# Gate products placed between the small products of the chunks' solve, in a fixed order on TensorE

## The chip, the cores and the metric

The kernel runs on one core of one Trainium2 chip. The metric is the device time of one execution in microseconds (us); lower is better. The core's engines are TensorE (PE in the profile; its weight loads are listed as PEld), VectorE (DVE), ScalarE (ACT), GpSimd (POOL) and SyncE (SP), which issues the transfers. Each engine takes its instructions in a fixed order and waits for others through semaphores.

## The reference, cut to what matters

The program computes two layers one after the other on 512 tokens of 1024 features. The change lies in the second one, in the branch of RWKV-7 time mixing and in the gates of the same layer:

```python
def step(state, inp):
    r_t, w_t, k_t, v_t, kk_t, a_t = inp
    sa = jnp.einsum('bhij,bhj->bhi', state, -kk_t)
    state = (state * w_t[:, :, None, :]
             + sa[..., None] * (kk_t * a_t)[:, :, None, :]
             + v_t[..., None] * k_t[:, :, None, :])
    return state, jnp.einsum('bhij,bhj->bhi', state, r_t)
...
y_a = rwkv7_branch(z_rw, shift_mu, ...)
...
g_a, g_b = jnp.split(jax.nn.sigmoid(z_gate + b_gate), 2, axis=-1)
```

The gates multiply the outputs of the branches much later. Their projection `z_gate` has 16 panels of 128 features; it depends on the normed input alone, so its products may stand anywhere ahead of that.

## The kernel before

The recurrence over 512 tokens is done in eight chunks of 64 tokens, for four pairs of heads. Within a chunk it is a lower triangular system. `rwkv_prep` builds the matrices `Mt` and the values `VA` in SBUF. `rwkv_solve` solves the systems of all chunks at once, ahead of the scan: diagonal blocks of 32x32 are written to DRAM and read back so that each partition holds one block (`NT`), 31 steps on VectorE (L1385, L1387) invert them all, the inverses go back through DRAM (`zdd`) into `Wm` and `Mt`, and then TensorE joins the halves. That last part is the solve of this document: four groups of sixteen 32x32 products (L1407), four more of them (L1415), each followed by a copy out of PSUM, and for each of the four pairs of heads 32 products of 64x64 (L1421 and L1424 in turn). L1363, 16 such products, prepares the fourth pair's right side. `rwkv_scan` then goes through the eight chunks one after the other (L1460, L1464, L1469, L1478 on TensorE, L1462, L1474, L1476 on VectorE), and `rwkv_out` follows.

A product of fp32 is made of three: `panel` loads a panel of weights (two transfers of 256 KB, `wraw`), ACT casts its high part (L125), GpSimd subtracts for its low part (L128), and `mm3` (L135) multiplies high by high, by low, and low by high. For a panel of gates that is 8 x 3 = 24 products of 128x512 into one PSUM bank `f`; ACT's tanh (L2181) takes it out and SP stores it to `gtd` (L2182).

The order is made by a scheduler of the tile framework from the order in which the code is written. `K.fills` marks products as filling: they have a low priority and are put wherever TensorE would wait. Eight gate panels (`G2_AHEAD`) are such fills, every fourth through pool `fw` and the rest with `'main'`, written behind `dsa_index`, the choice of keys for the sparse attention branch. In that choice L1557/L1558 multiply on TensorE, `mask` is made on VectorE (L1563 to L1566) and its largest entries are taken in rounds of eight (L1569, L1570). `dg` (L178) and its four transposes (L1578) belong to it too. The other eight gate panels and the products of the cross attention's memory are fills as well, written later. Pool `fw` has two buffers for filling panels (`how=True`); with `'main'` a panel takes one of the main pool's three.

Of the kernel before, what the change touches and what calls it, by code (L numbers as in the profile page):

```python
# [11 lines left out]
F32 = mybir.dt.float32  # L12
F32R = mybir.dt.float32r
I32 = mybir.dt.int32
AF = mybir.ActivationFunctionType
# [3 lines left out]
P = 128  # L19
# [4 lines left out]
G2_AHEAD = 8  # L24
DI_BUFS = 6
# [20 lines left out]
class Core:  # L46
# [90 lines left out]
    def fills(self, items, hi, lo, n=T, how=True):  # L137

        self.filling = how
        for src, done in items:  # L140
            done(self.fm(src, hi, lo, n))
        self.filling = False

# [1208 lines left out]
def rwkv_solve(K, pool, Mt, VA, Wm):  # L1352

    nc, tc, a = K.nc, K.tc, K.a
    nd = tc.dram_tile([P, 1024], F32, name="ndd")
# [45 lines left out]
    Q = Wm.rearrange("p i c t -> p i (c t)")  # L1401
    for i in range(4):
        pq = K.acc(tags[i])
        for s in range(2):
            for c in range(8):
                o = (s * 8 + c) * 32
                nc.tensor.matmul(pq[96:128, o:o + 32], Mt[64:96, i, s, c, 32:64], T1[64:96, i, s, c], start=True,  # L1407
                                 stop=True, tile_position=(64, 96))
        K.copy(Q[96:128, i], pq[96:128])
    for i in range(4):  # L1410
        pz = K.acc(tags[i])
        for s in range(2):
            for c in range(8):
                o = (s * 8 + c) * 32
                nc.tensor.matmul(pz[64:96, o:o + 32], Q[96:128, i, o:o + 32], Mt[96:128, i, s, c, 32:64], start=True,  # L1415
                                 stop=True, tile_position=(96, 64))
        K.copy(Mt[64:96, i, :, :, 32:64], pz[64:96].rearrange("p (s c t) -> p s c t", s=2, c=8))
    for i in range(4):
# [8 lines left out]
        for c in range(8):  # L1427
            two(0, c)
            one(0, c)
            two(1, c)  # L1430
            one(1, c)
# [708 lines left out]
def block2(K, h3, xd, out):  # L2140
# [22 lines left out]
    K.dve_split = ()  # L2163
    DS = ExitStack()
# [5 lines left out]
    rwkv_solve(K, K.pool(I_, "inv"), Mt, VA, Wm)  # L2170
# [7 lines left out]
    def gate(f):  # L2178
        def done(z):
            t = rp.tile([P, 512], F32, name="gt", bufs=2)  # L2180
            nc.scalar.activation(t, z, AF.Tanh, scale=0.5, bias=K.pd["bg"][:, f:f + 1])  # L2181
            nc.sync.dma_start(gtd[f], t)  # L2182
        return done

    idx = dsa_index(K, dp, hhi, hlo)
    for f in range(G2_AHEAD):
        K.fills([(a["w2f"][22 + f], gate(f))], hhi, hlo, how=f%4==0 or 'main')
# [208 lines left out]
```

## Time and profile before

| | us |
|---|---|
| median of 3 runs | 2240.3 |
| lowest and highest run | 2227.89, 2240.66 |
| profiled execution | 2238.75 |
| its span, first to last instruction | 2237.0 |
| PE busy | 2086.9 (93%) |
| DVE busy | 1074.4 (48%) |
| ACT busy | 712.5 (32%) |
| POOL busy | 485.6 (22%) |
| chain that ended last: PE, DVE, DMA | 68%, 12%, 7% |
| granted TensorE clock over the span | 0.965 |

Busy time of TensorE counts records with modelled ends, and products overlap, so a rate is better read from the starts of successive instructions than from their lengths. [...] An fp32 product of the small kinds has two records.

The stages of interest are at these times of the span: the inverse on VectorE ends at about 1186 us, the solve's small products stand between 1208 and 1251, the scan from there to 1293.

### The profile page before, as it was taken

The page shows a single profiled execution, that of the slowest core. Times are in us where ns is not written, and L with a number is a line of the kernel's source. Part 1 is how long each engine was busy: PE and PEld are TensorE (multiplying, and loading weights), DVE is VectorE, ACT ScalarE, POOL GpSimd, SP SyncE. Part 2 cuts the span into 40 slices and gives each one's busy share as a digit, 9 for nine tenths or more (in the row PEclk, how much of TensorE's full clock was granted, in tenths as well). Part 3 has the DMA queues.
Part 4 walks back from the last instruction along what each step waited for, and adds up shares of the span by engine and source line. Part 5 has one row for each costly group of instructions (what it writes and reads, how often), then busy time and mean ns, then how long its engine had stood idle before and what let it go on. Part 6 is the DMA issues. An engine that isn't in the chain of part 4 may idle for free.

```text
span 2237.0 us, 28592 instructions
## 1 busy us (share of the span) xinstructions
PE 2086.9 (93%) x10252; PEld 1476.5 (66%) x10252; DVE 1074.4 (48%) x2554; ACT 712.5 (32%) x1507; POOL 485.6 (22%) x391
## 2 busy tenths in 40 slices
PE   7999899998999999979988999999997999999997
PEld 5777676686888888867777867777875433333332
DVE  5272226427764545475877656555445322222223
ACT  4253334433353434234532235543441110000102
POOL 2312331233133222233331121232131000000000
PEclk9899999999999999999998799999998999999999
DMA  5512332256242332133334342485257999999994
GB/s 174 162 47 67 94 97 73 67 173 230 73 138 96 98 99 95 58 112 107 101 116 108 105 162 91 156 260 167 94 187 264 403 416 413 413 415 414 413 415 182
DMA packets 203370, 411.39 MB, mean 184 GB/s; under 512 B 49192, under 2 KB 67752, under 8 KB 203096
## 3 DMA queue, kind: packets, MB, share of 16 engines
q1 hardware_dynamic: 200632, 400.08, 51.0%
q0 software_dynamic: 2592, 9.44, 1.1%
q8 instruction: 82, 1.34, 0.3%
q14 instruction: 64, 0.52, 0.1%
HBM read 371.46 MB, written 33.13 MB: 181 GB/s over the span
## 4 chain that ended last, share of the span: by engine, by line
PE 68%; DVE 12%; DMA 7%; issue 3%; ACT 3%; POOL 2%; SPq 0%; DVEq 0%; ACTq 0%; POOLq 0%
PE f L135 23%; PE f L2008 10%; PE s L2024 6%; PE acc L135 6%; PE s L135 6%; PE tp L135 2%; POOL w L128 2%; PE pv L269 1%; PE tp L261 1%; PE s L1934 1%; DMA wraw<-w2f 1%; PE pv L135 1%; ACT w L125 1%; DMA wraw<-wout 1%; PE pv L1934 1%
## 5 line engine op out<-in xcount | busy, mean ns | idle before, releaser
L128 POOL TENSOR_TENSOR w<-wraw,w 128x512 fp32r<-128x512 f32 x310 | 407.2, 1325 | 1074.1 <-ACT w L125 962.0
L125 ACT CAST w<-wraw 128x512 fp32r<-128x512 f32 (+1 forms) x446 | 261.6, 617 | 242.2 <-issue 51.7
L135 PE MATMUL f<-hhi,w 128*128 128x512 f32 (+1 forms) x832 | 281.0, 410 | 2.0 <-ACT w L125 0.7
L128 DVE TENSOR_TENSOR w<-wraw,w 128x512 fp32r<-128x512 f32 (+1 forms) x136 | 116.3, 856 | 189.6 <-ACT w L125 186.5
L2008 PE MATMUL f<-mw,xT 128*64 128x512 f32 x832 | 206.8, 594 | 0.0
L135 PE MATMUL f<-h2hi,w 128*128 128x512 f32 (+1 forms) x672 | 203.7, 384 | 0.3 <-POOL w L128 0.3
L135 PEld LDWEIGHTS f<-hhi,w 128*128 128x128 f32 x832 | 161.8, 200 | 35.1 <-issue 3.2
L135 PE MATMUL acc<-hhi,w 128*128 128x512 f32 (+1 forms) x512 | 169.3, 398 | 4.9 <-ACT w L125 1.9
L135 PE MATMUL f<-hlo,w 128*128 128x512 f32 (+1 forms) x416 | 170.0, 409 | 0.2 <-DVE hlo L187 0.2
L2008 PEld LDWEIGHTS f<-mw,xT 128*64 128x64 f32 x832 | 65.5, 137 | 124.6 <-issue 117.7
L135 PEld LDWEIGHTS f<-h2hi,w 128*128 128x128 f32 x672 | 125.2, 188 | 25.6 <-POOL w L128 0.5
L135 PE MATMUL f<-h2lo,w 128*128 128x512 f32 (+1 forms) x336 | 129.0, 384 | 0.0
L2024 PE MATMUL s<-mw,hT 128*64 128x512 f32 x416 | 121.8, 600 | 3.3 <-ACT hT L174 1.9
L135 PEld LDWEIGHTS acc<-hhi,w 128*128 128x128 f32 x512 | 96.3, 191 | 28.5 <-issue 4.3
L1966 POOL DMA_INDIRECT xs<-xnd,row x16 | 15.2, 953 | 423.3 <-DVE wraw L2000 171.0
L135 PE MATMUL acc<-hlo,w 128*128 128x512 f32 (+1 forms) x256 | 101.3, 396 | 0.0
L135 PEld LDWEIGHTS f<-hlo,w 128*128 128x128 f32 x416 | 83.1, 200 | 16.2 <-issue 1.4
L1895 DVE SCALAR_TENSOR_TENSOR hid<-hid,f 128x512 f32<-128x512 f32 x16 | 11.0, 688 | 160.3 <-ACT hid L1894 160.3
L1894 ACT ACTIVATE hid<-f,tg 128x512 f32<-128x512 f32 x16 | 11.0, 688 | 204.1 <-PE f L2008 204.1
L2024 PEld LDWEIGHTS s<-mw,hT 128*64 128x64 f32 x416 | 33.2, 136 | 59.6 <-issue 51.5
L135 PEld LDWEIGHTS f<-h2lo,w 128*128 128x128 f32 x336 | 63.1, 188 | 12.3
L2027 ACT ACTIVATE yhi<-s,tg 128x512 fp32r<-128x512 f32 x32 | 22.0, 688 | 150.8 <-PE s L2024 150.8
(743 smaller groups left out, 3991.4 us busy)
## 6 DMA issues: line engine op xcount, KB each, us to landing
mw<-wexp SPq DMA_DIRECT2D x310, 512.0 KB
w<-wexp SPq DMA_DIRECT2D x72, 512.0 KB
wraw<-wup SPq DMA_DIRECT2D x88, 256.0 KB
wraw<-w2f SPq DMA_DIRECT2D x76, 256.0 KB
wraw<-wgate SPq DMA_DIRECT2D x64, 256.0 KB
wraw<-wdown SPq DMA_DIRECT2D x44, 256.0 KB
wraw<-w1f SPq DMA_DIRECT2D x40, 256.0 KB
gated<-gt SPq DMA_DIRECT2D x28, 256.0 KB
```

Of the source, the lines that this page charges most:

```text
L125: nc.scalar.copy(hi[:, s], raw)
L128: eng.tensor_sub(lo[:, s], raw, hi[:, s].bitcast(F32))
L135: self.nc.tensor.matmul(out, l, r, start=start and i == 0, stop=stop and i == 2)
L261: nc.tensor.transpose(pt[:, off:off + P], Pt[s][i][:, j * P:(j + 1) * P], K.ident)
L269: one = lambda s: nc.tensor.matmul(o[64 * s:64 * s + 64, j * P:], v_of(j, s), ptS[s][:, at[j]:at[j] + n], start=start and j == 0, stop=sto ...
L1894: nc.scalar.activation(t, G, AF.Tanh, scale=half)
L1895: nc.vector.scalar_tensor_tensor(t, t, 1.0, G, op0=OP.add, op1=OP.mult)
L1934: K.nc.tensor.matmul(o, CT[:, b * P:(b + 1) * P], y[:, hs], start=start and i == 0, stop=i == len(items) - 1)
L1966: nc.gpsimd.indirect_dma_start(xs, None, self.xnd, bass.IndirectOffsetOnAxis(ap=row[:, 0:1], axis=0))
L2008: nc.tensor.matmul(o[64 * s:64 * s + 64], xT[:, kk, 64 * s:64 * s + 64], ws[s][k], start=kk == 0, stop=kk == 7)
L2024: nc.tensor.matmul(o[64 * s:64 * s + 64], hT[:, c, 64 * s:64 * s + 64], ws[s][c], start=c == 0, stop=c == 3)
L2027: nc.scalar.activation(yhi[:, hs], o, AF.Copy, scale=tg[:, 1:2])
```

## The change

A generator, `K.steps`, takes six of the gate panels (`G2_SOLVE`) and gives out their products three at a time. `rwkv_solve` gets it as `fill`. It takes one step (three products) at its beginning, and its function `between` then issues the small products in groups of sixteen (L1407, L1415) or eight (L1421/L1424), each followed by two steps, which is six gate products. With `tc.issue_after` each group stands behind the last gate product and the gate products behind the last of the group, so that this order on TensorE is fixed. All of their panels are loaded through pool `fw` of two buffers, and split by ACT and GpSimd. Only two gate panels are still written as fills behind `dsa_index`.

```diff
@@ -22,6 +22,7 @@
 G2_BUFS = 7
 BD_BUFS = 2
 G2_AHEAD = 8
+G2_SOLVE = 6
 DI_BUFS = 6
 DG_BUFS = 10
 DB_BUFS = 8
@@ -140,6 +141,23 @@
         for src, done in items:
             done(self.fm(src, hi, lo, n))
         self.filling = False
+
+    def steps(self, items, hi, lo):
+
+        pans = []
+        for n, (src, done) in enumerate(items):
+            self.filling = True
+            pans += [self.panel(s, 1024) for s, _ in items[len(pans):n + 2]]
+            o = self.acc("f")
+            self.filling = False
+            for k in range(8):
+                s = slice(k * P, (k + 1) * P)
+                w = [t[:, s] for t in pans[n]]
+                for i, (a, b) in enumerate(((0, hi), (0, lo), (1, hi))):
+                    self.last = self.nc.tensor.matmul(o, w[a], b[:, k, :], start=k == 0 and i == 0, stop=k == 7 and i == 2)
+                if k == 7:
+                    done(o)
+                yield
 
     def acc(self, name="acc"):
         if name not in self.pb:
@@ -1349,9 +1367,21 @@
         nc.sync.dma_start(kbd[:, :, p].rearrange("c p t -> p c t"), KB)
 
 
-def rwkv_solve(K, pool, Mt, VA, Wm):
+def rwkv_solve(K, pool, Mt, VA, Wm, fill):
+
 
     nc, tc, a = K.nc, K.tc, K.a
+    next(fill)
+
+    def between(products, n):
+        for i in range(0, len(products), n):
+            with tc.issue_after(K.last.ins):
+                for p in products[i:i + n]:
+                    K.last = p()
+            with tc.issue_after(K.last.ins):
+                next(fill, None)
+                next(fill, None)
+
     nd = tc.dram_tile([P, 1024], F32, name="ndd")
     zd = tc.dram_tile([P, 2, 1024], F32, name="zdd")
 
@@ -1399,21 +1429,18 @@
                                       ap=[[32, 32], [4096, 64], [1, 32]]))
     tags = ("acc", "pv", "s", "s")
     Q = Wm.rearrange("p i c t -> p i (c t)")
+    at = [(s, c, slice((s * 8 + c) * 32, (s * 8 + c) * 32 + 32)) for s in range(2) for c in range(8)]
     for i in range(4):
         pq = K.acc(tags[i])
-        for s in range(2):
-            for c in range(8):
-                o = (s * 8 + c) * 32
-                nc.tensor.matmul(pq[96:128, o:o + 32], Mt[64:96, i, s, c, 32:64], T1[64:96, i, s, c], start=True,
-                                 stop=True, tile_position=(64, 96))
+        between([lambda s=s, c=c, o=o: nc.tensor.matmul(pq[96:128, o], Mt[64:96, i, s, c, 32:64], T1[64:96, i, s, c],
+                                                        start=True, stop=True, tile_position=(64, 96))
+                 for s, c, o in at], 16)
         K.copy(Q[96:128, i], pq[96:128])
     for i in range(4):
         pz = K.acc(tags[i])
-        for s in range(2):
-            for c in range(8):
-                o = (s * 8 + c) * 32
-                nc.tensor.matmul(pz[64:96, o:o + 32], Q[96:128, i, o:o + 32], Mt[96:128, i, s, c, 32:64], start=True,
-                                 stop=True, tile_position=(96, 64))
+        between([lambda s=s, c=c, o=o: nc.tensor.matmul(pz[64:96, o], Q[96:128, i, o], Mt[96:128, i, s, c, 32:64],
+                                                        start=True, stop=True, tile_position=(96, 64))
+                 for s, c, o in at], 16)
         K.copy(Mt[64:96, i, :, :, 32:64], pz[64:96].rearrange("p (s c t) -> p s c t", s=2, c=8))
     for i in range(4):
 
@@ -1424,11 +1451,7 @@
         two = lambda s, c: nc.tensor.matmul(pu[s][64:128, c * 64:(c + 1) * 64], Mt[64:128, i, s, c, 0:64],
                                             LV[i][64:128, s, c * 64:(c + 1) * 64], start=True, stop=True,
                                             tile_position=(64, 64))
-        for c in range(8):
-            two(0, c)
-            one(0, c)
-            two(1, c)
-            one(1, c)
+        between([lambda f=f, s=s, c=c: f(s, c) for c in range(8) for f, s in ((two, 0), (one, 0), (two, 1), (one, 1))], 8)
         K.copy(Wm[:, i].rearrange("p c t -> p (c t)"), pw)
         for s in range(2):
             K.copy(VA[64:128, i, :, 64 * s:64 * s + 64], pu[s][64:128].rearrange("p (c t) -> p c t", c=8))
@@ -2161,13 +2184,24 @@
     rwkv_prep(K, K.pool(S, "prep"), hhi, hlo, Mt, VA, eC, xg, kbd, red, bvd)
     S.close()
     K.dve_split = ()
+
+    def gate(f):
+        def done(z):
+            t = rp.tile([P, 512], F32, name="gt", bufs=2)
+            nc.scalar.activation(t, z, AF.Tanh, scale=0.5, bias=K.pd["bg"][:, f:f + 1])
+            nc.sync.dma_start(gtd[f], t)
+        return done
+
     DS = ExitStack()
     dp = K.pool(DS, "dsa", "left")
     V = ExitStack()
     vp = K.pool(V, "solve")
     Wm = vp.tile([P, 4, 8, 64], F32, name="Wm")
     I_ = ExitStack()
-    rwkv_solve(K, K.pool(I_, "inv"), Mt, VA, Wm)
+    fill = K.steps([(a["w2f"][22 + f], gate(f)) for f in range(G2_SOLVE)], hhi, hlo)
+    rwkv_solve(K, K.pool(I_, "inv"), Mt, VA, Wm, fill)
+    for _ in fill:
+        pass
     I_.close()
     rwkv_scan(K, K.pool(V, "scan"), Mt, VA, Wm, eC, kbd, red, ytd)
     V.close()
@@ -2175,15 +2209,8 @@
     U = ExitStack()
     rwkv_out(K, K.pool(U, "rout"), xg, ytd, bvd, yad)
     U.close()
-    def gate(f):
-        def done(z):
-            t = rp.tile([P, 512], F32, name="gt", bufs=2)
-            nc.scalar.activation(t, z, AF.Tanh, scale=0.5, bias=K.pd["bg"][:, f:f + 1])
-            nc.sync.dma_start(gtd[f], t)
-        return done
-
     idx = dsa_index(K, dp, hhi, hlo)
-    for f in range(G2_AHEAD):
+    for f in range(G2_SOLVE, G2_AHEAD):
         K.fills([(a["w2f"][22 + f], gate(f))], hhi, hlo, how=f%4==0 or 'main')
     DA = ExitStack()
     datt = K.pool(DA, "datt")
```

The first place is the index products on TensorE (L1557/L1558, `tp<-dg,qv`; L1580/L1581 in the changed file), which stand while VectorE works on the inverse. `f<-hhi,w` and `f<-hlo,w` are products of gate panels. Before:

```order
3181 L135 MATMUL f<-hhi,w 128x512
3182 L135 MATMUL f<-hlo,w 128x512
3183 L135 MATMUL f<-hhi,w 128x512 x2
3184 L135 MATMUL f<-hlo,w 128x512
3185 L1557 MATMUL tp<-dg,qv 128x512
3186 L1558 MATMUL tp<-dg,qv 128x512
3187 L135 MATMUL f<-hhi,w 128x512 x2
3188 L135 MATMUL f<-hlo,w 128x512
```

And with the change, at the end of the same index products:

```order
3193 L1580 MATMUL tp<-dg,qv 128x256
3194 L1581 MATMUL tp<-dg,qv 128x256
3195 L1580 MATMUL tp<-dg,qv 128x256
3196 L1581 MATMUL tp<-dg,qv 128x256
3197 L136 MATMUL tp<-hhi,w 128x512
3198 L136 MATMUL tp<-hlo,w 128x512
3199 L136 MATMUL tp<-hhi,w 128x512 x2
3200 L136 MATMUL tp<-hlo,w 128x512
```

The gate products between the index products are gone; the next full-width products are those of the branch's own panel, into `tp`.

The second place is the beginning of the solve on TensorE (L1407; L1435 in the changed file). Before:

```order
3322 L135 MATMUL f<-hhi,w 128x512 x2
3323 L135 MATMUL f<-hlo,w 128x512
3324 L135 MATMUL f<-hhi,w 128x512 x2
3325 L135 MATMUL f<-hlo,w 128x512
3326 L1407 MATMUL acc<-Wm,Mt 32x32 x16
3327 L1407 MATMUL pv<-Wm,Mt 32x32 x16
3328 L1407 MATMUL s<-Wm,Mt 32x32 x32
3329 L135 MATMUL f<-hhi,w 128x512 x2
```

And with the change:

```order
3213 L136 MATMUL tp<-hhi,w 128x512
3214 L1601 MATMUL tp<-ident,dg 128x128 x4
3215 L1435 MATMUL acc<-Wm,Mt 32x32 x16
3216 L157 MATMUL f<-hhi,w 128x512
3217 L157 MATMUL f<-hlo,w 128x512
3218 L157 MATMUL f<-hhi,w 128x512 x2
3219 L157 MATMUL f<-hlo,w 128x512
3220 L157 MATMUL f<-hhi,w 128x512
3221 L1435 MATMUL pv<-Wm,Mt 32x32 x16
```

The run of gate products ahead of the small ones is gone, the four transposes (L1578; L1601) stand right ahead of them, and six gate products follow each group.

The third place is VectorE in the scan, where L1462 (L1485 in the changed file) updates `VA`, and L1474, L1476 (L1497, L1499) the state `S`. L1569 and L1570 are a selection round on `mask`. Before:

```order
1307 L1462 TENSOR_TENSOR VA<-VA,s 64x4x128
1308 L1569 MAX m_10249<-mask_10193 128x8
1309 L1570 MATCH_REPLACE mask_10193<-m_10249,mask_10193 128x256
1310 L1569 MAX m_10252<-mask_10193 128x8
1311 L1474 TENSOR_TENSOR S_9539<-S_9540,acc 64x4x64 x2
1312 L1476 TENSOR_TENSOR S_9539<-S_9539,eC 64x4x64 x2
1313 L1570 MATCH_REPLACE mask_10193<-m_10252,mask_10193 128x256
```

And with the change:

```order
1313 L1485 TENSOR_TENSOR VA<-VA,s 64x4x128
1314 L1497 TENSOR_TENSOR S_9761<-S_9762,acc 64x4x64 x2
1315 L1499 TENSOR_TENSOR S_9761<-S_9761,eC 64x4x64 x2
1316 L1485 TENSOR_TENSOR VA<-VA,s 64x4x128
1317 L1497 TENSOR_TENSOR S_9762<-S_9761,acc 64x4x64 x2
```

The rounds that stood in the scan now stand in the solve, between its copies.

## Rows read from the trace of the kernel before

**Rows 1.** Windows: stretch and its length, busy time and count by engine, clock, DMA.

```profile
core 0: us, PE busy (x) PEld busy (x) DVE busy (x) ACT busy (x) POOL busy (x), PEclk, DMA share, GB/s
1148.00:1208.00 60.00, 50.21 (x204) 39.50 (x202) 59.15 (x131) 18.53 (x41) 19.25 (x15) 0.92 0.43 117
1208.00:1225.00 17.00, 17.00 (x279) 14.68 (x278) 7.48 (x18) 3.00 (x5) 0.00 (x0) 0.80 0.36 107
1225.00:1251.00 26.00, 26.00 (x301) 24.88 (x299) 8.05 (x15) 7.02 (x12) 5.97 (x6) 0.51 0.20 69
1251.00:1292.00 41.00, 38.94 (x258) 33.60 (x258) 32.11 (x88) 8.64 (x21) 5.06 (x4) 0.94 0.36 110
1292.00:1600.00 308.00, 289.75 (x1539) 232.20 (x1537) 173.84 (x404) 134.76 (x311) 79.15 (x61) 0.99 0.51 163
96.00:116.00 20.00, 20.00 (x72) 17.86 (x72) 2.69 (x11) 1.93 (x5) 1.27 (x1) 0.50 0.20 69
```

**Rows 2.** Timeline of TensorE: start, length, instruction, count, idle before and its releaser.

```profile
1201.54 1.09 PE L1578 MATMUL tp<-ident,dg 128*128 128x128 f32 x4 [2.06 <-DVE dg L178]
...
1208.28 1.19 PE L1407 MATMUL acc<-Wm,Mt 32*32 32x32 f32 x32
1209.31 1.17 PE L1407 MATMUL pv<-Wm,Mt 32*32 32x32 f32 x32
...
1225.17 0.61 PE L1421 MATMUL acc<-Mt,VA 64*64 64x64 f32 x9
```

**Rows 3.** Timeline of TensorE in the inverse: gate products at either level.

```profile
1165.44 0.62 PE L135 MATMUL f<-hhi,w 128*128 128x512 f32 x2
...
1166.12 0.62 PE L135 MATMUL f<-hhi,w 128*128 128x512 f32 x2
...
1185.41 0.63 PE L135 MATMUL f<-hhi,w 128*128 128x512 f32 x1
1185.84 0.63 PE L135 MATMUL f<-hlo,w 128*128 128x512 f32 x1
```

**Rows 4.** The chain that ended last, pieces in the solve: start, length, what.

```profile
1232.09 2.73 PE s L1363 x26
...
1245.02 2.00 PE f L135 x4
...
1250.62 1.15 PE f L135 x2
```

**Rows 5.** TensorE by line and form, 1148 to 1208: count, busy, mean ns.

```profile
L135 PE MATMUL f<-hhi,w 128*128 128x512 f32 x101 | 34.4, 417 | 0.0
L135 PE MATMUL f<-hlo,w 128*128 128x512 f32 x51 | 21.2, 416 | 0.0
```

**Rows 6.** Timelines of VectorE, GpSimd and ACT beside the inverse.

```profile
1164.70 0.37 DVE L1385 TENSOR_TENSOR ztmp<-Z,NT 128x220 f32<-128x220 f32 x1
...
1166.56 1.43 DVE L1385 TENSOR_TENSOR ztmp<-Z,NT 128x207 f32<-128x207 f32 x1
...
1179.41 0.70 DVE L1387 TENSOR_TENSOR Z<-Z,ztmp 128x112 f32<-128x112 f32 x1
...
1199.24 0.89 DVE L1566 TENSOR_TENSOR mask<-mask,dmask 128x128 f32<-128x128 f32 x1
...
1166.46 2.68 POOL L128 TENSOR_TENSOR w<-wraw,w 128x512 fp32r<-128x512 f32 x2 [8.29 <-ACT w L125]
...
1165.77 1.13 ACT L125 CAST w<-wraw 128x512 fp32r<-128x512 f32 x2
```

**Rows 7.** Timeline of TensorE in the scan: the first products of four steps.

```profile
1275.05 1.16 PE L1460 MATMUL s<-S,Wm 128*128 128x128 f32 x8 [0.26 <-DVE S L1476]
...
1280.56 1.16 PE L1460 MATMUL s<-S,Wm 128*128 128x128 f32 x8 [0.26 <-DVE S L1476]
...
1285.85 1.16 PE L1460 MATMUL s<-S,Wm 128*128 128x128 f32 x8
...
1290.81 1.16 PE L1460 MATMUL s<-S,Wm 128*128 128x128 f32 x8
```

## Prediction

> **What bounds the kernel now.** I read the windows of the profile first, because the change sits in one stage. In them the reader sees TensorE busy 50.2 of 60 us in the last part of the DVE inverse (1148 to 1208), and 17.0 of 17 and 26.0 of 26 us in the two halves of the solve, but at a granted clock of 0.80 and 0.51 there [rows 1]. [...] Then I read TensorE's timeline: the products of L1407 start at 1208.28 right behind gate products, without a wait, and the last thing TensorE did wait for was 2.06 us for the DVE copy `dg` ahead of L1578, at 1201.54 [rows 2]. So until 1201 VectorE ends last, from there to 1251 TensorE does, and in the scan the two take turns.
>
> **Prices of TensorE's work.** Three gate products start every 0.68 us at the full level, so one is 0.227 us and six are 1.36; at the low level one is 0.43, six are 2.56 [rows 3]. Sixteen products of L1407 are 32 records, 1.03 us at the full level [rows 2]. At the low level I take twice that, 2.06. From 1225.17 [rows 2] to the gate products at 1250.62 stand 128 products of L1421/L1424, the 16 of L1363 (26 of their 32 records take 2.73 us, so 3.4 for all) and four gate products (2.00) [rows 4]: 25.45 - 3.4 - 2.0 = 20.05 us, or 1.25 for eight at the low level. The trace has no such group at the full level; half is 0.63. The bounds are 0.52 (L1407's pace of 1.03 for sixteen) and 1.25 (no gain).
>
> **What is taken out of the wait.** In 1148 to 1208 TensorE ran 101 + 51 recorded gate products [rows 5], 152 x 0.227 = 34.5 us, while it would otherwise have waited for VectorE. In the new order none stands there: the 24 index products and the 24 of `fm` go back to back. The wait is now really idle, and nothing takes it over. As to the path, that is no loss by itself, since VectorE ends last there.
>
> **What VectorE gains.** The inverse's two-input products (L1385, L1387) are stretched whenever GpSimd splits a panel: 1.43 us for 207 columns where 220 took 0.37 a little earlier, and it happens beside GpSimd's pair of splits at 1166.46 [rows 6], the first of three such pairs. The six stretched ones, from 1.43 at 1166.56 to 0.70 at 1179.41, sum to 5.54 us [rows 6], where I estimate 1.86 undisturbed from the neighbours of 0.37 and less: 3.7 us. Behind the inverse four more mask operations are stretched, 2.5 us in all, the last at 1199.24, 0.89 us for 128 columns [rows 6]; there one panel's split still stands in the new order, and I take half, 1.2. VectorE passes the same number of operations between the inverse's end and the `dg` copy as before. So L1578 starts at 1201.54 - 4.9 = 1196.6, and the solve, 0.74 us behind it, at 1197.4 instead of 1208.28. The bounds are 6.2 us (1196.1) and nothing (1202.3). The block transfers that the solve reads were issued behind the inverse too and move with it, so they don't end last.
>
> **The solve, at the full level.** Eight groups of sixteen with six gate products each: 8 x (1.03 + 1.36) = 19.1. Sixteen groups of eight: 16 x (0.63 + 1.36) = 31.8, and L1363 1.7. It ends at 1197.4 + 52.6 = 1250.0, where it ended at 1250.6 [rows 4]: -0.6 us. Panels come through a pool of two buffers. The third is split behind the first one's tanh, on ACT (two casts, 1.13 us) and GpSimd (2.68 for two) [rows 6], with the tanh about 4.5 us, while the second panel's 24 products with their small groups last 9.6 or 8 us. Three to five us are to spare, so I cost the loads at nothing; a panel that is late costs its own lateness, since TensorE's order is now fixed.
>
> **What is left over.** Up to the scan the order has 202 full-width `f` products before and 151 after, 51 fewer: 51 x 0.227 = 11.6 us that stand later, behind the scan. There TensorE idles 308 - 289.75 = 18.3 us [rows 1], but in many short waits whose places the order fills as before; I let 3 us of the 11.6 vanish (bounds 0 and 11.6). The scan starts at the full level rather than the low one (clock 0.94 in 41 us [rows 1] is 4.9 us at half speed, 2.5 us to win). And the scan's steps lose their selection rounds on VectorE: 5.51 us with them, 4.96 without [rows 7], 0.55 over four to five steps, 2.5 us.
>
> Sum at the full level: -0.6 + 11.6 - 3 - 2.5 - 2.5 = +3.0 us. Against the profiled execution's own 2238.75 us (1.6 below the median of 2240.3) that is 2241.8.
>
> **The clock is the open term.** A stretch of the same make stands early in the program: from 96 to 116 narrow products alternate with two or three gate-sized ones, TensorE is busy 20.0 of 20 us, and the clock stays at 0.50 all the time [rows 1]. In the scan, which follows on the second half of the solve at 0.51 and has four gate products a step, the clock was 0.94 on the mean [rows 1]. So a mixture seems to keep whichever level it has. What is the level at the entry? TensorE waits again for `dg` ahead of L1578, as it did for 2.06 us before. By my times `fm` begins cold about 1185, ends about 1194, and waits some 2.5 us. In the kernel before, the products behind that wait ran low (1.09 us for four [rows 2], and gate products 0.43 apart) and a dense run of twenty gate products brought the clock back. Now sixteen small products follow instead, and then only six gate products at a time. I think the low entry likelier than the full one. At the low level a group of the first stage costs 2.06 + 2.56 - 2.39 = 2.23 us more, and one of the second 1.25 + 2.56 - 1.99 = 1.82.
>
> [...]
>
> **The likeliest case (B).** The clock enters low, comes back somewhere in the first stage, where the six gate products make up over half of each group's time, and is held from there: four groups at 2.23 give 8.9 us. 2241.8 + 8.9 = 2250.7; I say 2250. Chance 0.25, with its own range of 2244 to 2257.
>
> **Rivals.**
> - A: full level throughout, 2242. For it: dense `fm` products stand right ahead of the entry. Against it: the wait for `dg`. Chance 0.25.
> - C: the first stage stays low and the second, with its denser share of gate products, comes up: 8 x 2.23 = 17.8, so 2259.6 (A's 2241.8 and 17.8). Half of it is over 1% above. Chance 0.15.
> - D, the slower side: the mixture never comes up, as in 96 to 116. The price is 17.8 + 16 x 1.82 + 1.7 for L1363 + the 2.5 of the scan's start = 51 us: 2293. It decides if the clock is low at the entry and the gate products' share in a group is too thin. Against it: that share is larger here than in 96 to 116. Chance 0.2.
> - E: the later idle takes all of the 11.6 us, and the entry is full: -0.6 + 0 - 2.5 - 2.5 - 1.3 (all of the stretching gone) = -6.9, 2232; with more of the 18.3 us of later idle closed, as the selection masks are ready earlier, up to 1% less than before. For it: TensorE's waits there are for VectorE's results. Against it: the order fills the same places as before. Chance 0.15, of which 0.1 may lie below 1%.
>
> **How the numbers follow.** 1% of 2240 (22 us, about what a measurement can tell from no change) puts the limits at 2216 to 2218 and 2261 to 2263. Faster: 0.1 of E. Slower: D and two thirds of C, 0.3. Within: 0.6. The range takes all but the ends of D and E: 2228 to 2291. The one for B's case alone is above.
>
> **What would show each step.** In the changed kernel's profile: L1578 of before (the four transposes ahead of the solve) at about 1196.6, the first small products right behind it; no stretched products in the inverse beyond 1160; in the windows of the solve a clock near 1.0 (A, E), rising within 1197 to 1235 (B, C), or 0.5 until the scan (D); scan steps of 4.96 us throughout; TensorE idle some 30 us between 1148 and 1197; and about 56 more full-width gate products behind the scan. It is wrong if the panels come late (idle in TensorE's row ahead of gate products in the solve), if VectorE is not earlier at `dg`, or if the later stages swallow or double the 11.6 us.

## The result and the profile after

The changed kernel takes 2259.7 us (median of four runs, 2252.6 to 2265.8); the kernel before, measured beside it, takes 2240.3. The ratio is 1.0123, with a 95% interval of 1.0082 to 1.0163: some 1.2% slower (the two medians alone are 0.9% apart). Its profiled execution took 2259.7 us. Measured a second time (`e0_after` below), the ratio was 1.0133 (1.0082 to 1.0184).

| | before | after |
|---|---|---|
| span of the profiled execution, us | 2237.0 | 2257.9 |
| PE busy, us | 2086.9 | 2086.5 |
| PE idle, us | 150.1 | 171.4 |
| granted TensorE clock | 0.965 | 0.965 |

The page of the changed kernel, the span and the first row of part 1:

```profile
span 2257.9 us, 28602 instructions
PE 2086.5 (92%) x10252; PEld 1460.2 (65%) x10252; DVE 1068.3 (47%) x2554; ACT 714.0 (32%) x1507; POOL 486.2 (22%) x391
```

TensorE's busy time is what it was, so the time is not in added work but in when it is idle and how fast it runs. To see where, I divided both executions at the same instructions. Executions of the changed kernel and of variants of it that differ only behind this point stand up to 16 us apart where this stage begins (1100.1 to 1116.1 us), so the stages are measured from each other and not from the start. "Prep end" is the first product of L1363 (L1393 after), "transposes" are those of L1578 (L1601), "scan" is the first product of L1460 (L1483), "queries" the last products of the sparse attention's queries (L1635, L1658), "cross" the first product of the cross attention's scores (L1808 before). The predicted column is worked out from the prediction's terms, the 2.5 us of the scan's start counted to the second row.

| us from ... to ... | before | predicted | after |
|---|---|---|---|
| prep end, transposes | 82.3 | 77.4 | 73.0 |
| transposes, scan | 57.2 | 67.9 | 69.7 |
| scan, queries | 166.4 | | 162.7 |
| queries, cross | 175.0 | | 203.3 |
| the last two together | 341.4 | 347.5 | 366.0 |
| cross, end | 636.9 | 636.9 | 636.0 |

So the stage that was changed came out close to the forecast, the inverse better, and the loss stands 160 us behind the change, in the stretch between the sparse attention and the cross attention: 28.3 us more there.

The windows of the changed kernel, with the same columns as [rows 1]: the inverse's end, the solve, its end and the scan, and the two stretches behind.

```profile
1148.00:1180.00 32.00, 9.72 (x24) 6.76 (x25) 31.93 (x87) 4.18 (x10) 0.00 (x0) 0.50 0.26 60
1180.00:1208.00 28.00, 26.85 (x288) 20.83 (x287) 25.34 (x67) 6.94 (x18) 6.26 (x5) 0.85 0.30 73
1208.00:1225.00 17.00, 17.00 (x179) 12.95 (x178) 11.79 (x36) 5.80 (x10) 5.05 (x4) 1.00 0.25 83
1225.00:1251.00 26.00, 26.00 (x243) 19.42 (x243) 5.18 (x15) 5.45 (x10) 5.96 (x6) 1.00 0.29 98
1251.00:1275.00 24.00, 23.88 (x171) 21.06 (x172) 10.95 (x23) 4.98 (x13) 2.54 (x2) 1.00 0.45 132
...
1255.90:1418.60 162.70, 157.37 (x842) 118.32 (x842) 86.62 (x220) 66.38 (x149) 33.95 (x25) 1.00 0.38 122
1418.60:1621.90 203.30, 185.25 (x980) 153.09 (x979) 105.97 (x215) 79.04 (x183) 55.27 (x42) 0.96 0.58 185
```

And the same last stretch before, between the same two instructions:

```profile
1425.10:1600.10 175.00, 163.55 (x876) 137.98 (x875) 97.68 (x207) 72.35 (x170) 47.80 (x37) 0.98 0.58 186
```

The clock in the solve is 1.00 from 1208 on, behind a first part at 0.85, where [rows 1] has 0.80 and 0.51: this is what the gate products did (without them, in `e6_none` below, it is 0.73 from the transposes to the scan, where the changed kernel has 0.95). In the inverse TensorE now idles 22.3 of 32 us with VectorE busy 31.93. In the last stretch three things are worse at once: 104 more recorded products (980 against 876), 18.05 us of idle against 11.45, and a clock of 0.96 against 0.98.

TensorE's timeline in the changed kernel (columns as in [rows 2]): the inverse's end, the entry into the solve, one period of each stage, and two steps of the scan.

```profile
1172.47 0.58 PE L1580 MATMUL tp<-dg,qv 128*128 128x256 f32 x1 [19.34 <-ACT big L1584]
...
1186.19 0.63 PE L1601 MATMUL tp<-ident,dg 128*128 128x128 f32 x4 [1.15 <-DVE dg L196]
1186.74 1.19 PE L1435 MATMUL acc<-Wm,Mt 32*32 32x32 f32 x32
...
1190.48 1.91 PE L1435 MATMUL pv<-Wm,Mt 32*32 32x32 f32 x32
...
1195.13 1.19 PE L1435 MATMUL s<-Wm,Mt 32*32 32x32 f32 x32
1196.25 0.50 PE L157 MATMUL f<-hhi,w 128*128 128x512 f32 x1
...
1197.84 1.19 PE L1435 MATMUL s<-Wm,Mt 32*32 32x32 f32 x32
...
1213.87 0.27 PE L1451 MATMUL s<-LV,Mt 64*64 64x64 f32 x1
...
1214.70 0.50 PE L157 MATMUL f<-hhi,w 128*128 128x512 f32 x1
...
1216.30 0.27 PE L1451 MATMUL s<-LV,Mt 64*64 64x64 f32 x1
...
1255.91 1.13 PE L1483 MATMUL s<-S,Wm 128*128 128x128 f32 x8
1260.89 1.16 PE L1483 MATMUL s<-S,Wm 128*128 128x128 f32 x8
```

The four transposes (0.63 us) and the first group (1.19) still ran at the full level, a clock of 1.00 from 1186.19 to 1187.90. The second group's 1.91 us, where the third has 1.19, shows the low level (0.51 from 1188 to 1194); the third group starts 4.65 us behind the second, where a period at the full level is 2.71 (1195.13 to 1197.84). From there on nothing falls back until the scan (1.00 from 1195.13 to 1251.65). A scan step is 4.98 us. TensorE's idle row in the whole solve is the 1.15 us ahead of the transposes: no panel came late.

VectorE and GpSimd in the same inverse:

```profile
1157.85 0.36 DVE L1415 TENSOR_TENSOR ztmp<-Z,NT 128x207 f32<-128x207 f32 x1
```

```profile
1185.82 2.51 POOL L129 TENSOR_TENSOR w<-wraw,w 128x512 fp32r<-128x512 f32 x2 [39.26 <-ACT w L126]
```

The product with 207 columns that took 1.43 us before [rows 6] takes 0.36, and GpSimd has nothing to split for 39 us around it.

What stands in the last stretch, by line and form, after and then before (the products of the cross attention's memory into `f`; they are fills, 128x256 each):

```profile
L136 PE MATMUL f<-memhi,w 128*128 128x256 f32 x117 | 22.5, 287 | 0.2 <-DVE mkl L205 0.2
L136 PE MATMUL f<-memlo,w 128*128 128x256 f32 x58 | 16.6, 286 | 0.0
```

```profile
L135 PE MATMUL f<-memhi,w 128*128 128x256 f32 x47 | 9.7, 291 | 0.0
L135 PE MATMUL f<-memlo,w 128*128 128x256 f32 x24 | 7.1, 295 | 0.0
```

175 against 71. All 104 products that came into the stretch are of this kind, and none of them is a gate product. Where they came from stands in the stretch ahead, scan to queries, here by the rows of the high parts, before and then after:

```profile
L135 PE MATMUL f<-hhi,w 128*128 128x512 f32 x117 | 40.5, 412 | 0.0
L135 PE MATMUL f<-memhi,w 128*128 128x256 f32 x81 | 16.3, 290 | 0.0
```

```profile
L136 PE MATMUL f<-hhi,w 128*128 128x512 f32 x154 | 54.5, 416 | 0.0
L136 PE MATMUL f<-memhi,w 128*128 128x256 f32 x11 | 2.1, 282 | 0.0
```

With the low parts, 175 gate products became 231 there, and 121 memory products became 17. And what TensorE waits for behind the queries in the changed kernel (waits of PE in that stretch: total us, times, longest):

```profile
PE f L136 <- DVE mkl L205: 7.1, 4, 4.0
PE f L136 <- ACT w L126: 2.2, 3, 1.2
PE s L136 <- ACT w L126: 1.5, 1, 1.5
PE f L136 <- POOL w L129: 1.3, 2, 0.7
```

Waits for a panel's cast or split (`w`) sum to 8.7 us with five smaller rows; before, one such wait of 0.6 us stood in that stretch.

### The profile page after: what moved, and what is told of

Same layout as the page of the kernel before. It is cut to its first block, busy times and chain, and to the rows that moved or that the text cites. A ratio compares the mean times of both kernels' runs of the same rounds, so it can differ in the third digit from the quotient of the medians.

```text
span 2257.9 us, 28602 instructions
## 1 busy us (share of the span) xinstructions
PE 2086.5 (92%) x10252; PEld 1460.2 (65%) x10252; DVE 1068.3 (47%) x2554; ACT 714.0 (32%) x1507; POOL 486.2 (22%) x391
## 4 chain that ended last, share of the span: by engine, by line
PE 68%; DVE 11%; DMA 7%; issue 4%; ACT 4%; POOL 2%; SPq 0%; DVEq 0%; ACTq 0%; POOLq 0%
PE f L136 22%; PE f L2031 10%; PE s L2047 6%; PE acc L136 6%; PE s L136 5%; PE f L157 2%; PE pv L287 1%; PE tp L136 1%; POOL w L129 1%; PE tp L279 1%; ACT w L126 1%; PE s L1957 1%; DMA wraw<-wo 1%; PE pv L136 1%; PE pv L1957 1%
## 5 line engine op out<-in xcount | busy, mean ns | idle before, releaser
L136 PE MATMUL f<-hhi,w 128*128 128x512 f32 (+1 forms) x736 | 244.1, 402 | 2.1 <-ACT hhi L204 0.8
L136 PEld LDWEIGHTS f<-hhi,w 128*128 128x128 f32 x736 | 137.7, 193 | 31.1 <-issue 4.7
L136 PE MATMUL f<-hlo,w 128*128 128x512 f32 (+1 forms) x368 | 147.3, 401 | 0.2 <-DVE hlo L205 0.2
L136 PEld LDWEIGHTS f<-hlo,w 128*128 128x128 f32 x368 | 71.1, 193 | 13.8 <-issue 2.0
L136 PEld LDWEIGHTS f<-h2lo,w 128*128 128x128 f32 x336 | 63.1, 188 | 12.4
```

The costliest lines, as they stand in the source:

```text
L136: self.nc.tensor.matmul(out, l, r, start=start and i == 0, stop=stop and i == 2)
```

## The experiments

Two theories were set against each other at first. One puts the loss on the products that the change leaves over for later. Its rival puts it on the solve: the fixed order, or what the mixture itself costs. Later runs narrow the first. What a number of an expectation rests on is told in it. All ratios are against the kernel before measured beside each run, whose medians were 2229.4, 2226.3 and 2229.6 us. The expectations count from 2240.3 and 2259.7 us, and the kernel before stood 11 to 14 us lower beside these runs, so an expected time is compared through the ratio and not as it stands.

**The fixed order without its gate products.** As an edit of the changed kernel: no panel in the solve, all eight among the fills again, the small products in the changed kernel's groups and order:

```diff
-G2_SOLVE = 6
+G2_SOLVE = 0
...
-                next(fill, None)
-                next(fill, None)
```

> The change without its gate products: the small products are issued in the same fixed groups, but no gate product stands between them, and all eight panels are fills behind the index as before. Theories 1 and 2 both: TensorE's wait in the inverse is filled again, the solve runs at the low clock, 2238 to 2243, as before the change; the fixed order by itself costs nothing. If it were the fixed order that costs (groups waiting for each other's copies): over 2250.

Measured: 2231.3 us, ratio 0.9999 (0.9966 to 1.0031). No cost of the order by itself can be seen. Its windows at the transposes and in the solve:

```profile
1184.30:1235.30 51.00, 50.98 (x628) 46.42 (x629) 27.00 (x65) 13.66 (x30) 9.58 (x9) 0.73 0.28 87
```

Transposes to scan take 50.9 us at a mean clock of 0.73, with 63 gate products among them. That is 14.3 us at 0.227 each, so the rest of the stage is 36.6. In the changed kernel 151 gate products stand in it (141 of the solve's, 10 fills behind them), 34.3 us, and the rest is 69.7 - 34.3 = 35.4. Counted so, the full clock has won only 1.2 us. But the kernel before, with 63 gate products too, was longer at the low level in its profiled execution than this run (a clock of 0.64 in that stage): its rest is 57.2 - 14.3 = 42.9. What the clock won depends on which execution it is counted against.

**Fewer gate products in the mixture.** Three panels, and three products behind each group in place of six:

```diff
-G2_SOLVE = 6
+G2_SOLVE = 3
...
                 next(fill, None)
-                next(fill, None)
```

> The changed kernel with half the gate products in the solve: three panels instead of six, three products behind each group instead of six; the other five panels of the eight are fills behind the index. Theory 1 (the share of gate products keeps the clock): the share falls from over a half to about a third of a group's time, the clock is low in most of the solve (below 0.7 from the first group to the scan); the solve lasts 75 us or more although 16 us of work are gone from it (69.7 from the four transposes to the scan's first product in the changed kernel), and the 72 products come later at full price: 40 us or more above the kernel before. Theory 2 (any gate products between are enough): the solve lasts 50 to 55 us at a clock near 1.0, and the time is that of the changed kernel, about 27 us above the one before.

Measured: 2271.8 us, ratio 1.0194 (1.0146 to 1.0241), with 80.7 us from the transposes to the scan, as the first theory had it. Windows in its solve:

```profile
1177.27:1186.50 9.23, 9.23 (x174) 7.39 (x173) 8.71 (x22) 2.30 (x10) 1.86 (x2) 1.00 0.26 85
1186.50:1254.80 68.30, 68.30 (x457) 50.07 (x457) 27.84 (x77) 11.91 (x21) 9.72 (x9) 0.50 0.12 42
1255.00:1270.00 15.00, 14.92 (x109) 13.01 (x108) 6.28 (x13) 1.82 (x5) 0.00 (x0) 1.00 0.46 141
```

TensorE is never idle in these windows of the solve. It entered at the full level, fell after 9 us, without a wait ahead of the fall, and stayed at a clock of 0.50 for 68 us, until the scan. So what stands between the small products made the difference: with three wide ones per group the clock fell and stayed down in this execution; with six, a fall in the changed kernel's solve was over after 6.8 us. The prediction's cases B and D differed in just this.

**Half as many changes between small and wide.** The same products as in the changed kernel, 32 small and twelve gate products at a time in the first stage, sixteen and twelve in the second:

```diff
-    def between(products, n):
+    def between(products, n, steps):
...
-                next(fill, None)
-                next(fill, None)
+                for _ in range(steps):
+                    next(fill, None)
...
-                 for s, c, o in at], 16)
+                 for s, c, o in at], 16, 4 * (i % 2))
...
-        between([...], 8)
+        between([...], 16, 4)
```

> The changed kernel with twelve gate products behind each second group instead of six behind each, nothing else. Theory 1 (a change between small and gate products costs about 0.4 us): 12 changes less, 4 to 6 us below the changed kernel. Rival (longer runs of small products let the clock fall): no gain, or a loss of up to 15 us.

> The changed kernel unaltered, beside the next two on the same chip. By the first comparison (ratio 1.0123) and by its profile from the end of the preparation on, 27 us above the kernel before.

Measured: 2247.9 us, 1.0077 (1.0051 to 1.0102), beside the changed kernel itself with 2260.6, 1.0133. The medians are 12.7 us apart, the two profiled executions 3.6 (spans 2258.0 and 2261.6), and the two intervals overlap, so the gain in total is not settled. In the stage it is: transposes to scan take 63.4 us, at a clock of 0.97, against 66.8. Two more executions with the changed kernel's solve (`e3_after_less` and `e7_after_nomem`, below) took 66.9 and 66.8; only the first one took 69.7. Its window of that stage and then that of `e0_after` say why:

```profile
1186.19:1255.91 69.72, 69.72 (x716) 53.47 (x716) 38.32 (x102) 19.78 (x42) 19.43 (x17) 0.95 0.27 87
```

```profile
1189.54:1256.30 66.76, 66.76 (x715) 51.44 (x716) 38.34 (x102) 20.05 (x42) 19.72 (x17) 1.00 0.28 90
```

The clock fell in the first execution and in none of the other three, which are at 1.00 from the transposes to the scan. With 34.3 us of gate products their rest is 32.5. TensorE's timeline in `e9_wide`:

```profile
1200.29 1.19 PE L1441 MATMUL acc<-Mt,Wm 32*32 32x32 f32 x32
1201.33 1.17 PE L1441 MATMUL pv<-Mt,Wm 32*32 32x32 f32 x32
1202.43 0.50 PE L157 MATMUL f<-hhi,w 128*128 128x512 f32 x1
...
1205.42 0.75 PE L1441 MATMUL s<-Mt,Wm 32*32 32x32 f32 x18
...
1210.56 0.27 PE L1451 MATMUL s<-LV,Mt 64*64 64x64 f32 x1
...
1215.10 0.27 PE L1451 MATMUL s<-LV,Mt 64*64 64x64 f32 x1
```

One period here holds what two hold in the changed kernel. It takes 5.13 us (1200.29 to 1205.42) where two take 2 x 2.715 = 5.43, and 4.54 (1210.56 to 1215.10) where two take 2 x 2.435 = 4.87. One round trip between small and wide products therefore costs 0.30 and 0.33 us, and the solve makes 24 of them: 8 x 0.30 + 16 x 0.33 = 7.7 us. The products themselves follow too: six wide ones more take (1205.42 - 1202.43) - (1197.84 - 1196.25) = 1.40 us, 0.233 each, and eight 64x64 take 4.54 / 2 - 1.40 less half a round trip (0.16), 0.71. These rows show that a change costs, and how much; what in it costs, they do not show. The prediction has no such term.

**The filling of the inverse given back.** The gate panels 6 to 10 are written inside `rwkv_solve`, ahead of the 31 steps and at a lower priority, and the solve's first step behind them:

```diff
+G2_INV = 5
+G2_AHEAD = G2_SOLVE + G2_INV + 2
...
-    next(fill)
...
+    ahead()
+    next(fill)
...
+    def ahead():
+        for f in range(G2_SOLVE, G2_SOLVE + G2_INV):
+            with tc.high_priority(offset=-4000):
+                K.fills([(a["w2f"][22 + f], gate(f))], hhi, hlo)
```

> The change with one addition: five more gate panels (6 to 10) are written ahead of the inverse as fills of low priority, so that their PSUM banks are given out before those of the six panels in the solve; TensorE's wait in the inverse is filled again, and the two fills behind the index are panels 11 and 12. Theory 1 (work left behind: the 20 us are products that lost their place in the inverse's wait and now stand behind the sparse attention, where nothing covers them): five panels x 24 x 0.227 = 27 us less stand there, minus 3 to 6 us that GpSimd's splits give back to VectorE's inverse; 2259.7 - 21 to 24 = 2236 to 2239, or a few us below if the full clock in the solve is kept. Theory 2 (the later stage itself is disturbed: the waits for the memory's panels and the low clock behind 1434 us are the loss, whatever work is left): 2250 to 2260.

Measured: 2245.3 us, 1.0071 (1.0045 to 1.0096). The wait is full again (114 gate products between the prep's end and the transposes, where the kernel before has 138 and the changed one none), and the stretch between queries and cross takes 178.0 us, with 32 memory products: back near the 175.0 of before, as the first theory had it. But the solve takes 79.8 us from the transposes to the scan. Two rows of TensorE's timeline say why:

```profile
1183.91 0.63 PE L1603 MATMUL tp<-ident,dg 128*128 128x128 f32 x4 [3.10 <-DVE dg L197]
...
1215.40 0.80 PE L158 MATMUL f<-hhi,w 128*128 128x512 f32 x1 [4.03 <-ACT gt L2193]
```

The entry waits 3.10 us and runs low behind it (a clock of 0.57 from 1184 to 1200). And 4.03 us are lost to the tanh of a panel (L2193), which holds the bank `f` that the next one needs. On ACT that tanh stands at 1214.66, behind a cast that waited for a transfer:

```profile
1213.42 0.62 ACT L1641 CAST dg<-dg 128x512 fp32r<-128x512 f32 x1 [5.04 <-DMA dg<-w_ukT]
...
1214.66 1.30 ACT L2193 ACTIVATE gt<-f,ppd 128x512 f32<-128x512 f32 x2
```

By the ratio the total is 16 us above the kernel before, where the first theory had 1 to 4 below and the second 10 to 20 above: the stretch came out as the first had it, the total as the second. What is won behind is lost in front.

So the wait can be filled. That the changed kernel does not fill it is a matter of the order in which its products are written. By the code, the two PSUM banks named `f` are given out in that order: the first of the solve's panels is opened long ahead of the inverse (its first three products stand at 1017.5 us, the next at 1187.9), and a fill that is written behind the six gets a bank only when they end. That it is the banks, and not another buffer, is argued and was not tested apart.

**The two together, and with fewer panels.** Fills in the inverse as just above and half as many changes, first with five panels, then with `G2_INV = 3`:

> As e1_low5 (five more panels as low fills in the inverse's wait), but the six panels of the solve stand twelve products behind each second group instead of six behind each: half as many changes between small and gate products. Theory 1 (a change between them costs: a period of 2.72 us where the parts give 2.39, and 2.43 where they give 1.99): 12 changes less at about 0.4, 5 us below e1_low5, which stood 16 us above the kernel before: 11 above. Rival (the longer runs of small products, 2 us, let the clock fall): as e1_low5 or slower, 16 us or more above.

> As e10_low5_wide with three panels instead of five in the inverse's wait, so that about as many gate products stand ahead of the scan as in the kernel before (nine panels; before 8.4). If the work left behind the scan sets the end: what is taken out of the wait comes back later at full price, 48 x 0.227 = 11 us above e10_low5_wide (0.65% above before), 25 us above before. If the slots between the scan and the end of the sparse attention were short of fills in e10_low5_wide, so that its two panels more brought nothing: as e10_low5_wide, 10 to 15 us above before. Level with the kernel before would show that the mixture is free once the wait is filled.

Measured: 2241.8 us, 1.0065 (1.0038 to 1.0093), and 2239.2 us, 1.0029 (1.0003 to 1.0055). With five panels the total, 8 to 21 us above the kernel before, decides neither for the 11 nor for the 16 us. The stage from the transposes to the scan takes 74.6 us, 5 less than above, and the same wait for the tanh is there again, 4.88 us long, behind 5.59 us of ACT's waiting for that transfer:

```profile
1222.16 0.79 PE L158 MATMUL f<-hhi,w 128*128 128x512 f32 x1 [4.88 <-ACT gt L2193]
```

With three panels the stages are 78.0, 64.8, 163.2 and 179.8 us: the best of the mixtures, and by its interval (1 to 12 us above) still not below the kernel before. The 25 us above are excluded, 10 to 15 are only just possible, and level, which would have shown the mixture to be free, it is not either.

**Less work left over.** In the changed kernel the two panels still written behind `dsa_index` are cut to their first three products each, 42 products or 9.5 us of work left out; in the kernel before the same two panels (`fm_short` is `fm` with the first of its eight steps alone):

```diff
-        K.fills([(a["w2f"][22 + f], gate(f))], hhi, hlo, how=f%4==0 or 'main')
+        K.filling = f%4==0 or 'main'
+        gate(f)(K.fm_short(a["w2f"][22 + f], hhi, hlo))
+        K.filling = False
```

> The changed kernel with 42 products left out: of the two gate panels that are still written as fills behind the index (6 and 7) only three of 24 products are made, so those gates are not computed. Theory 1: a product taken out of the queue of fills shortens its end, where nothing covers it: 42 x 0.227 = 9.5 us, 2250. Theory 2: the end of the queue waits for other things, the saving is under 3 us: 2257 or more.

> The kernel before with the same 42 products left out (panels 6 and 7, three of 24 products each). Theory 1: here too a product less in the queue shortens its end, as TensorE is busy 93%: 2240.3 - 9.5 = 2231. Theory 2: in this order the waits cover them: 2237 or more.

Measured: 2235.8 us, 1.0017 (0.9992 to 1.0041), and 2224.1, 0.9981 (0.9950 to 1.0011). By the ratios the same work is worth 4 us before, which is not clear of nothing (and so decides between neither of its theories), and over 20 in the changed kernel, from 1.0123 or 1.0133 down to 1.0017. From the prep's end to the end the profiled executions show less: 15 us in the changed kernel (1144.8 to 1129.6) and 6 in the one before (1117.8 to 1111.9). By stages queries to cross fall from 203.3 to 189.1, with 84 memory products in place of 175. In the changed kernel left-over work costs more than its own length, and more than either theory gave it.

**The memory's products left out of both.** The same cut in the eight panels of the memory's keys, 168 products of 128x256, in the changed kernel and in the one before:

```diff
-    K.fills([(a["wck"][i], lambda o, i=i: out(lambda w: kTd[:, w, i], o[:, :256])) for i in range(8)], mhi, mlo, 256, "mixed")
...
+    for i in range(8):
+        o = K.fm_short(a["wck"][i], mhi, mlo, 256)
+        out(lambda w: kTd[:, w, i], o[:, :256])
```

> The changed kernel with 168 products of 128x256 left out: of the eight panels of the memory's keys only three of 24 products are made (their panels are still loaded and split). Behind the sparse attention stood 175 products of 128x256 in the changed kernel's profile, 71 in the one before. Theory 1a (all of the loss there is the products' own time and what they disturb): the stretch from the sparse attention's last query products to the cross attention shrinks from 203 to 177 or less, and the time stands within 5 us of the kernel before with the same products left out. Theory 1b (the loss is the supply of panels, which then come one upon the other: waits for ACT and GpSimd and a low clock): the stretch keeps 10 us or more above that of the other run, 185 to 190, and so does the time.

> The kernel before with the same 168 products of 128x256 left out (panels of the memory's keys still loaded and split). Both theories: 19 us of work less; what stood behind the sparse attention (71 products, 8 us) is saved, the rest stood under waits or lets later fills move up: 8 to 19 us below the kernel before, the stretch to the cross attention 165 to 170.

Measured: 2233.2 us, 1.0042 (1.0013 to 1.0070), and 2225.5, 0.9994 (0.9966 to 1.0022). The kernel before did not become 8 to 19 us faster by it, as was expected. The difference between the two orders shrinks from 27 to about 10 us, but 186.0 against 168.9 remain from queries to cross, as theory 1b had it. I first read this as a cost that has nothing to do with the left-over products. The rows by line and form in that stretch, of the changed kernel's variant and then of the other's, say otherwise:

```profile
L136 PE MATMUL f<-w,memhi 128*128 128x512 f32 x64 | 22.1, 423 | 3.9 <-DVE mkl L212 3.9
L136 PE MATMUL f<-w,memlo 128*128 128x512 f32 x32 | 13.6, 425 | 0.0
```

```profile
L135 PE MATMUL f<-w,memhi 128*128 128x512 f32 x43 | 14.8, 408 | 0.4 <-DVE mkl L194 0.4
L135 PE MATMUL f<-w,memlo 128*128 128x512 f32 x22 | 9.0, 408 | 0.0
```

With the keys' products gone, the next in the queue of fills, the memory's other panels, are pushed out: 31 more full-width products, and 23 narrower ones. That is 31 x 0.227 + 23 x 0.113 = 9.6 of the 17.1 us. Leaving work out of a queue that fills waits moves the whole queue up; it does not take one cause away.

## Why the prediction was right in the stage and wrong behind it

The measured time lies in the range of 2228 to 2291, 10 us above the 2250 and 3 above the range of case B, and by the ratio of 1.2% a little outside of "within 1%", which had 6 chances in 10. (Half of C is above 1% in one place of the prediction and two thirds in another; with half, slower had 0.275 and not 0.3.) That it came so near is partly luck: from the prep's end on the profile shows 26.9 us more, where the terms give 11.9, and the profiled execution stood 6.0 us ahead when that stage began. One of the prediction's own signs of being wrong is there: the later stages more than doubled the 11.6 us. Its terms went like this.

**VectorE's gain: right in kind, too small.** 4.9 us were predicted, and the transposes come 9.3 us earlier after the prep's end. The stretched products behind 1166 gave the 3.7 us that I estimated: from the product with 220 columns (1164.70 before [rows 6], 1156.00 after) to the last with 31 (1183.72 and 1171.32) it is 19.0 against 15.3. What I had not read lies on both sides of that: 2.7 us earlier in the inverse, and 2.9 behind it, where I had taken 1.2.

**The clock: case B in the first execution, rival A's level in three others.** In the profile of the result the clock was full at the entry, fell behind the first group, came back within the first stage, and was held: near B, but not low at the entry. The cost was smaller than 8.9 us: the first two groups took 3.74 and 4.65 us, where 2.71 is a period at the full level, so 3.0. In `e0_after`, `e3_after_less` and `e7_after_nomem`, with the same solve, the clock was 1.00 throughout, as A has it; "I think the low entry likelier than the full one" did not hold. The wait for `dg` ahead of the transposes was 1.15 us in the first and 0.88 in the others, where some 2.5 were expected; why the clock fell in one and not in the others is open. A's time is not right for it: at the full level transposes to scan take 66.8 us, where A's terms give 59.0 (67.9 less 8.9). Rival C has a whole stage at the low level. That the measured 2259.7 is C's 2259.6 is chance.

**A group's price: the mis-sized term.** Periods of 2.71 and 2.43 us stand where I had 2.39 and 1.99, so 8 x 0.32 + 16 x 0.44 = 9.6 us more. Of that 7.7 are the round trips measured above; the rest is eight 64x64 products at 0.71 instead of 0.63 and a gate product at 0.233. I had priced each kind by a row in which it stands among its own, and these rows cannot show what a change between them costs. The cheaper clock (5.9 us) takes back over half of it: the solve from its first small product to its last gate product lasted 64.9 us (1186.74 to 1251.65), where 52.6 + 8.9 = 61.5 were predicted.

**Panels and scan: right.** No gate product in the solve waits for its panel. The scan's steps stand 4.96 to 4.98 us apart throughout, and the scan starts at a clock of 1.00. Scan to queries is 3.7 us shorter, and all of that is idle time (8.9 us before, 162.70 - 157.37 = 5.3 after); 2.5 were predicted. The idle time in the inverse is there too, 31.0 us from the prep's end to the transposes (12.4 before).

**"I let 3 us of the 11.6 vanish": the step that failed.** I took 51 products too many behind the scan, 11.6 us, as something that the many short waits would half swallow, with bounds of 0 and 11.6. Up to the queries at most the 1.2 us beyond the 2.5 were swallowed, and behind them the upper bound was passed: 28.3 us more from queries to cross. Three parts of it can be read off:

- 104 more memory products at 0.113 us: 11.8. The 56 more gate products between scan and queries (175 to 231) took the places that 104 memory products had filled before (121 to 17), and these now stand where there is no wait to fill.
- Idle 18.05 against 11.45: 6.6. The largest waits are for the memory's own low part (7.1 against 4.7) and for panels' casts and splits (8.7 against 0.6).
- The clock, 0.96 of 203.3 us against 0.98 of 175.0: 8.1 - 3.5 = 4.6 us of lost full speed, an estimate from clocks of two digits.

Together 23.0; some 5 us are left without a row to put them to. A second execution of the changed kernel (`e0_after`) repeats the stretch: 206.0 us with the same 980 products, 18.6 us of idle and a clock of 0.94. That the first part causes the others was not shown: the run with fills in the inverse has only 32 memory products there and still waits more than the kernel before (12.9 us of idle, a clock of 0.96), as does `e6_none` (13.4 us of idle). That the left-over work as a whole is the cause is shown from two sides. With the wait filled again and the mixture kept (`e1_low5`) the stretch is back at 178.0 us, the same as without the mixture (177.9 in `e6_none`). And with 42 gate products fewer the ratio of 1.0017 lies outside the changed kernel's interval.

The prediction's rival E went by the same short waits and had them take everything; it was wrong for the same reason. The waits between scan and queries held 8.9 us of idle in all; the rest of them was filled already. A count of them by line (what fills each now, and what that displaces) was to be had from the trace before.

The sum by terms: predicted -4.9 + 10.7 + 6.1 = +11.9 us; by stages -9.3 + 12.5 - 3.7 + 28.3 - 0.9 = +26.9. The profiled execution shows 20.9, because it came to the prep's end 6.0 us earlier than the one before, in a part that both kernels share.

## What to carry to other kernels

Work that fills waits is a queue: when it is taken out of one wait, ask what it displaces in the next, and follow that to the first place where there is no wait left; there it is paid in full, with its panels' loads. A mixture of small and wide products held the clock at 1.00 here with six wide ones behind each group (from 1195.13 to 1251.65 in the changed kernel), but not with three (0.50 for 68 us in `e5_thin`), and each round trip between the two was paid with 0.30 to 0.33 us; groups twice as long, with twelve wide ones, held it as well (1.00 from 1195 to 1251 in `e9_wide`). The stage without its gate products at 0.227 us took 36.6 to 42.9 us in unmixed executions, 32.5 to 35.4 in those of the changed kernel's solve, and 30.4 with half the changes (`e9_wide`). That gain did not make up for the filled wait that was given up.

## What the hardware showed that I had not expected

A round trip between 32x32 or 64x64 products and 128x512 ones cost 0.30 to 0.33 us of TensorE at a clock of 1.00, by the periods of `e9_wide` and of the changed kernel. A mixture with three wide products per group (`e5_thin`) fell from a clock of 1.00 to 0.50 with TensorE busy without a gap, and stayed there for 68.30 of 68.30 busy us. With six per group, in four executions of the changed kernel's solve, it fell in one, was back within 9 us of the solve's beginning (1186.74 to 1195.13), and held 1.00; in the other three it did not fall.
